# A batched expert MLP on one Trainium2 core: x by one transfer of 32 KB rows, prepared by quarter of its columns and token parity

## The chip, the cores and the metric

The kernel runs on one core of one Trainium2 chip. The metric is the device time of one execution in microseconds (us), the median of several executions. TensorE (PE) multiplies, ScalarE (ACT) and VectorE (DVE) copy, cast and apply relu, GpSimd (POOL) and SyncE (SP) issue the transfers here.

## The reference

```python
# n_experts 8, capacity 256, hidden 512, expert_hidden 2048; all float32
def reference(x, w1, w2):            # x [8,256,512], w1 [8,512,2048], w2 [8,2048,512]
    h = np.matmul(x, w1)
    h = np.maximum(h, 0)
    return np.matmul(h, w2).astype(np.float32)
```

The weights are 67.1 MB of float32, x and the output 4.19 MB each. The kernel multiplies in bfloat16.

## The kernel before

Each expert has two weight matrices of 4.19 MB. GpSimd loads each by one transfer (the last w2 by two, of 9 and 7 of its 16 rows per partition), and the transfer casts float32 to bfloat16: one row of 32 KB of float32 for each of 128 partitions. There are two buffers for w1 (`w1_sb`) and two for w2 (`w2_sb`), one for even and one for odd experts.

The experts go in pairs. For a pair TensorE does layer 1 of the even expert, layer 1 of the odd one, then layer 2 of the even and of the odd one. Layer 1 of an expert is 128 matmuls into `ph` (L272); ACT and DVE take turns to apply relu into `ht` (L219, L221). Layer 2 is 32 matmuls into `po` (L292), which ACT and DVE copy to `o_sb` (L228).

The order of transfers is GpSimd's program. First come the third single expert of x (expert 3, L142), x of experts 4 to 7 with a cast (`x_c`, L143), w1 of experts 0 and 1, w2 of experts 0 and 1. Then, for each later pair, it waits until layer 1 of an expert is through (`s_first`, L161) and reloads that w1 buffer, and until layer 2 of an expert is copied out (`s_act`, L164) and reloads that w2 buffer. So w1 of expert 2 is issued when layer 1 of expert 0 has ended, and all that GpSimd issues stands in one queue in this order. At the end GpSimd writes the output of experts 0 to 3 (L167), and SyncE that of 4 to 6 and of 7 (L126, L128). SyncE also tells TensorE when weights are there (`t_w`, L106 to L124): for the first layers it waits until x of that expert is prepared (`s_xe`) and until w1 has landed.

x must have its hidden dimension on the partitions. This is done before the first layer, in four rounds. In a round DVE (b=0) and ACT (b=1) each cast 128 tokens' worth of rows, 1024 elements in each partition, into `x_b` (`cast`, L178); TensorE transposes 16 blocks of 128x128 into `pt` (L256); DVE and ACT each copy 1024 elements in each partition from `pt` into `xe` (L194, L198). A round's transposes wait for both casts, a copy for its eight transposes, and the next cast of an engine stands behind its copy. One round prepares two experts, so the first layer of expert 0 needs the first round alone; but TensorE's program has the four rounds ahead of all layers.

x comes by four transfers: expert 0 (512 KB, SyncE), experts 1 and 2 (1 MB, SyncE), expert 3 (512 KB, GpSimd), all float32 in `x_f`, and experts 4 to 7 (2 MB of float32, landing as bfloat16 in `x_c`, GpSimd). In each partition the rows of a transfer are 4, 8, 4 and 16 KB of float32. The copies to `xe` write runs of contiguous elements for experts 0 and 3 (L194), every second element for 1 and 2, every fourth for 4 to 7 (L198).

Of the kernel before, what the change touches and what calls it, by code (L numbers as in the profile page):

```python
# [9 lines left out]
def kernel(  # L10
# [7 lines left out]
    nc = tc.nc  # L18
    P = 128
    bf = mybir.dt.bfloat16  # L20
    f32 = mybir.dt.float32
    relu = mybir.ActivationFunctionType.Relu

    E, C, H = x.shape
    F = w1.shape[2]
    MT = C // P
    KT1 = H // P
# [3 lines left out]
    G = E // 2  # L31
# [6 lines left out]

    J = G * MT
    x_r = x.rearrange("e (p m) k -> p e m k", m=MT)
    x_pair = x[1:3].rearrange("e c k -> (e c) k").rearrange("(p s m) k -> p s m k", p=P, m=MT)
    x_rows = x[G:].rearrange("e c k -> (e c) k").rearrange("(p j) k -> p j k", p=P)


    x_f = nc.alloc_sbuf_tensor("x_f", [P, G, MT, H], f32)
    x_c = nc.alloc_sbuf_tensor("x_c", [P, J, H], bf)
    x_b = nc.alloc_sbuf_tensor("x_b", [P, 2, KT1 * MT, P], bf)
    xe = nc.alloc_sbuf_tensor("xe", [P, E * KT1 * C], bf)  # L50
    w1_sb = nc.alloc_sbuf_tensor("w1_sb", [P, 2 * KT1 * F + KT2], bf)
# [9 lines left out]
    pt = [nc.alloc_psum_tensor(f"pt_tr{b}", [P, KT1 * MT, P], bf) for b in range(2)]  # L61

    sem = nc.alloc_semaphore
    s_x = [sem(f"s_x{i}") for i in range(3)]
    s_xc = sem("s_xc")
    s_out = [sem(f"s_out{i}") for i in range(3)]
    s_w1 = [sem(f"s_w1_{e}") for e in range(E)]
    s_w2 = [sem(f"s_w2_{e}") for e in range(E)]
# [10 lines left out]
    t_xb = sem("t_xb")  # L79
    s_xe = [sem(f"s_xe{b}") for b in range(2)]  # L80
# [4 lines left out]
    sp, pool, act, dve, pe = nc.sync, nc.gpsimd, nc.scalar, nc.vector, nc.tensor  # L85
# [3 lines left out]

    def load_x(eng, e, n, src, i):
        ins = eng.dma_start(x_f[:, e:e + n], src).then_inc(s_x[i], 16)
        return ins.ins.name

    tc.no_tile_sem_insts.add(load_x(sp, 0, 1, x_r[:, :1], 0))
    tc.no_tile_sem_insts.add(load_x(sp, 1, 2, x_pair, 1))
    tc.close()
    tc.compile()  # L99

    def copied(eng, n):
        eng.wait_ge(s_act, n)
        eng.wait_ge(s_dve, n)


    for e in range(0, E, 2):  # L106
        for b in range(2):

            if e < G:
                sp.wait_ge(s_xe[b], e // 2 + 1)  # L110
                if e + b == 1:
                    sp.wait_ge(s_xe[0], 2)
            elif e + b == G:
                for s in s_xe:
                    sp.wait_ge(s, G)
            sp.wait_ge(s_w1[e + b], 16).then_inc(t_w, 1)
        for b in range(2):
            if b:
                copied(sp, e + 1)
            if e + b < E - 1:  # L120
                sp.wait_ge(s_w2[e + b], 16).then_inc(t_w, 2)
            else:
                sp.wait_ge(s_w2[e + b], 16).then_inc(t_w, 1)
                sp.wait_ge(s_w2b, 16).then_inc(t_w, 1)  # L124
# [6 lines left out]
    def load_w1(e):  # L131
        pool.dma_start(w1_k[:, e % 2 * KT1:(e % 2 + 1) * KT1], w1_r[e]).then_inc(s_w1[e], 16)  # L132

    def load_w2(e):
# [3 lines left out]
        else:  # L138
            pool.dma_start(w2_k[:, k:k + CUT], w2_r[e, :, :CUT]).then_inc(s_w2[e], 16)  # L139
            pool.dma_start(w2_k[:, k + CUT:k + KT2], w2_r[e, :, CUT:]).then_inc(s_w2b, 16)  # L140

    load_x(pool, G - 1, 1, x_r[:, G - 1:G], 2)  # L142
    pool.dma_start(x_c[:], x_rows).then_inc(s_xc, 16)  # L143
    load_w1(0)
    load_w1(1)
    pool.memset(identity[:], 0.0).then_inc(s_id, 1)
# [23 lines left out]

    def cast(eng, r, b):

        a = 2 * r + b
        src = x_f[:, a] if a < G else x_c[:, MT * (a - G):MT * (a - G + 1)]
        copy = act.copy if eng is act else dve.tensor_copy
        copy(  # L178
            x_b[:, b].rearrange("p (t m) q -> p t m q", m=MT),
            src.rearrange("p m (q t) -> p t m q", t=KT1),  # L180
        ).then_inc(t_xb, 1)

    def take_x(eng, b):
        copy = act.copy if eng is act else dve.tensor_copy
        for r in range(G):
            if r < G // 2:
                eng.wait_ge(s_x[(2 * r + b + 1) // 2], 16)
            elif r == G // 2:
                eng.wait_ge(s_xc, 16)
            cast(eng, r, b)  # L190
            eng.wait_ge(s_tr, 2 * r + b + 1)
            a, n = 2 * r + b, KT1 * C
            if a in (0, G - 1):
                copy(xe[:, a * n:(a + 1) * n], pt[b][:].rearrange("p j q -> p (j q)")).then_inc(s_xe[b], 1)  # L194
            else:
                e0, l = (1, 2) if a < G else (G, G)
                xl = xe[:, e0 * n:(e0 + l) * n].rearrange("p (l j q f) -> p l j q f", l=l, j=KT1 * MT, f=l)
                copy(  # L198
                    xl[:, :, :, :, a - e0].rearrange("p l j q -> p j l q"),
                    pt[b][:].rearrange("p j (l q) -> p j l q", l=l),  # L200
                ).then_inc(s_xe[b], 1)

# [25 lines left out]

    act.sem_inc(t_ha, 1)
    take_x(act, 1)
    layers(act, 1, s_ha, s_oa, t_ha, s_act)

    dve.sem_inc(t_hb, 1)
    take_x(dve, 0)
    layers(dve, 0, s_hb, s_ob, t_hb, s_dve)

# [13 lines left out]
    with pe.Fori(0, G) as _r:  # L252
        take(t_xb, 2)
        for b in range(2):
            for j in range(KT1 * MT):
                ins = pe.transpose(pt[b][:, j], x_b[:, b, j], identity[:])  # L256
            ins.then_inc(s_tr, 1)

    with pe.Fori(0, G) as g:
        with pe.Fori(0, 2) as b:  # L260
            xs = ahead(xe, False, g * (4 * KT1 * C) + b * (2 * KT1 * C), [kt * C for kt in range(KT1)], C)
            take(t_w)
            with pe.Fori(0, NQ) as q:
                for i in range(FB):
# [6 lines left out]
                    for kt in range(KT1):  # L271
                        ins = pe.matmul(  # L272
                            ph[i // 2][:, i % 2, :],
                            ws[i % 2 * KT1 + kt],
                            xs[kt],
                            start=(kt == 0),
                            stop=(kt == KT1 - 1),
                        )
                    if i % 2:
                        ins.then_inc((s_hb, s_ha)[i // 2], 1)  # L280
        with pe.Fori(0, 2) as b:
            for kt in range(KT2):
# [8 lines left out]
                for m in range(MT):  # L291
                    ins = pe.matmul(  # L292
                        po[:, m],
                        hs[(kt - k0) * MT + m],
                        ws[kt - k0],
                        start=(kt == 0),
                        stop=(kt == KT2 - 1),
                    )
# [35 lines left out]
```

## Time and profile before

| | |
|---|---|
| time of three executions | 179.56, 179.69, 179.77 us; median 179.69 |
| span of the profiled execution | 178.3 us, so 1.4 us of the median lie outside it |
| mean granted TensorE clock | 0.966 of full speed |
| PE, ACT, DVE busy | 73%, 21%, 21% of the span |
| read from and written to HBM | 71.30 MB, 4.19 MB: 423 GB/s over the span |

The profile is of one execution; its own time is its span. Busy time is per engine. A share of DMA is the mean over 16 DMA engines. A transfer that casts is counted by the bytes that it writes, half of those that it reads, so 217 GB/s of a casting transfer are 433 GB/s of float32. Durations of DMA_DIRECT2D are those of issuing; the time "to landing" runs from the issue to the arrival of the last byte.

### The profile page before, as it was taken

Reading aid. Unit: us, or ns where it says so; the run is one execution under the profiler, and the core shown is the slowest. Engines: PE = TensorE matmul, PEld = TensorE weight load, DVE = VectorE, ACT = ScalarE, POOL = GpSimd, SP = SyncE. Lnnn points to the kernel's source line nnn. Section 1 sums busy time; section 2 is a strip of 40 time slices with the busy share of each in tenths; the row PEclk is TensorE's granted clock in tenths of the full one; section 3 lists DMA queues with packets and bytes.
Section 4 is the critical chain, followed back from the end, with each engine's and each line's share of the span. In section 5 each row is a group of like instructions: output and inputs, shape, how many; then the busy total and the mean of one; then the engine's idle time right before and its main releaser. Section 6 shows DMA issues by size and latency. Waiting matters only on the chain. (4 is left out here: it accounts for less than half of the span.)

```text
span 178.3 us, 2360 instructions
## 1 busy us (share of the span) xinstructions
PE 130.5 (73%) x832; PEld 88.8 (50%) x832; DVE 37.6 (21%) x48; ACT 37.9 (21%) x49; POOL 12.3 (7%) x26
## 2 busy tenths in 40 slices
PE   0034479899939296888769695979496698999880
PEld 0033378785414195873224485954142587964330
DVE  0134654331010133330100231320101113410110
ACT  2455554232010122130100132220101022220110
POOL 3600000101010101000000101010101200000000
PEclk9999999999999999999969999999999569999997
DMA  5999999999999998998998998999999999999998
GB/s 232 327 217 224 235 198 213 235 202 210 235 213 198 235 221 191 235 224 191 232 228 191 228 232 191 224 232 202 213 235 202 210 235 213 198 218 208 270 421 353
DMA packets 4096, 40.90 MB, mean 229 GB/s; under 512 B 384, under 2 KB 384, under 8 KB 1792
## 3 DMA queue, kind: packets, MB, share of 16 engines
q0 software_dynamic: 3264, 37.23, 95.1%
q1 hardware_dynamic: 832, 3.67, 5.1%
HBM read 71.30 MB, written 4.19 MB: 423 GB/s over the span
## 5 line engine op out<-in xcount | busy, mean ns | idle before, releaser
L272 PE MATMUL pt_h<-xe,w_sb 128*128 x512 | 65.1, 283 | 13.0 <-PEq L88 13.0
L272 PEld LDWEIGHTS pt_h<-xe,w_sb 128*128 x512 | 57.4, 147 | 21.3 <-issue 19.5
L292 PE MATMUL pt_o<-w_sb,ht_sb 128*128 x256 | 58.2, 387 | 11.9 <-PEq L88 11.8
L292 PEld LDWEIGHTS pt_o<-w_sb,ht_sb 128*128 x256 | 24.9, 99 | 44.2 <-issue 16.9
L221 DVE TENSOR_SCALAR ht_sb<-pt_h 128x512 bf16<-128x512 f32 x32 | 22.2, 692 | 52.0 <-PE pt_h L272 52.0
L219 ACT ACTIVATE ht_sb<-pt_h 128x512 bf16<-128x512 f32 x32 | 19.2, 600 | 57.0 <-PE pt_h L272 57.0
L256 PE MATMUL pt_tr<-identity,x_b 128*128 128x128 bf16 x64 | 7.5, 309 | 17.8 <-PEq L88 17.8
L228 DVE COPY out_sb<-pt_o 128x512 f32 x8 | 5.5, 691 | 67.2 <-PE pt_o L292 67.2
L228 ACT COPY out_sb<-pt_o 128x512 f32 x8 | 4.7, 585 | 65.4 <-PE pt_o L292 65.4
L256 PEld LDWEIGHTS pt_tr<-identity,x_b 128*128 128x128 bf16 x64 | 6.5, 143 | 18.5 <-issue 18.5
L132 POOL DMA_DIRECT2D w_sb<-in_w_dram x8 | 4.9, 612 | 70.1 <-ACTq L223 70.1
L198 DVE COPY xe<-pt_tr 128x1024 bf16<-128x1024 bf16 x3 | 6.3, 2091 | 8.1 <-PE pt_tr L256 8.1
L198 ACT COPY xe<-pt_tr 128x1024 bf16<-128x1024 bf16 x3 | 6.3, 2085 | 6.1 <-PE pt_tr L256 6.1
L137 POOL DMA_DIRECT2D w_sb<-in_w_dram x7 | 3.7, 534 | 44.5 <-ACT out_sb L228 44.4
L178 ACT CAST x_b<-x_f 128x1024 bf16<-128x1024 f32 x2 | 4.0, 1984 | 3.0 <-DMA x_f<-in_x_dram 3.0
L178 DVE CAST x_b<-x_f 128x1024 bf16<-128x1024 f32 x2 | 2.1, 1064 | 4.1 <-DMA x_f<-in_x_dram 4.1
L178 ACT COPY x_b<-x_c 128x1024 bf16<-128x1024 bf16 x2 | 2.2, 1117 | 0.0
L178 ACT ACT_TABLE_LOAD x1 | 1.3, 1283 | 2.5 <-PEq L99 2.5
L194 DVE COPY xe<-pt_tr 128x1024 bf16<-128x1024 bf16 x1 | 0.7, 691 | 4.7 <-PE pt_tr L256 4.7
L194 ACT COPY xe<-pt_tr 128x1024 bf16<-128x1024 bf16 x1 | 1.0, 1012 | 2.0 <-PE pt_tr L256 2.0
L178 DVE COPY x_b<-x_c 128x1024 bf16<-128x1024 bf16 x2 | 1.4, 692 | 0.0
L139 POOL DMA_DIRECT2D w_sb<-in_w_dram x1 | 0.5, 528 | 9.2 <-ACT out_sb L228 9.2
(10 smaller groups left out, 3.4 us busy)
## 6 DMA issues: line engine op xcount, KB each, us to landing
w_sb<-in_w_dram POOLq DMA_DIRECT2D x15, 2048.0 KB, 29.9
out_dram<-out_sb POOLq DMA_DIRECT2D x1, 2048.0 KB, 35.9
out_dram<-out_sb SPq DMA_DIRECT2D x1, 1536.0 KB, 8.6
w_sb<-in_w_dram POOLq DMA_DIRECT2D x1, 1152.0 KB, 26.4
x_f<-in_x_dram SPq DMA_DIRECT2D x1, 1024.0 KB, 5.5
x_c<-in_x_dram POOLq DMA_DIRECT2D x1, 1024.0 KB, 9.3
w_sb<-in_w_dram POOLq DMA_DIRECT2D x1, 896.0 KB, 30.4
x_f<-in_x_dram SPq DMA_DIRECT2D x1, 512.0 KB, 3.3
```

The costliest lines, as they stand in the source:

```text
L132: pool.dma_start(w1_k[:, e % 2 * KT1:(e % 2 + 1) * KT1], w1_r[e]).then_inc(s_w1[e], 16)
L137: pool.dma_start(w2_k[:, k:k + KT2], w2_r[e]).then_inc(s_w2[e], 16)
L139: pool.dma_start(w2_k[:, k:k + CUT], w2_r[e, :, :CUT]).then_inc(s_w2[e], 16)
L178: copy(x_b[:, b].rearrange("p (t m) q -> p t m q", m=MT), src.rearrange("p m (q t) -> p t m q", t=KT1),).then_inc(t_xb, 1)
L194: copy(xe[:, a * n:(a + 1) * n], pt[b][:].rearrange("p j q -> p (j q)")).then_inc(s_xe[b], 1)
L198: copy(xl[:, :, :, :, a - e0].rearrange("p l j q -> p j l q"), pt[b][:].rearrange("p j (l q) -> p j l q", l=l),).then_inc(s_xe[b], 1)
L219: act.activation(dst, ph[half][:], relu).then_inc(t_h, 1)
L221: dve.tensor_relu(dst, ph[half][:]).then_inc(t_h, 1)
L228: copy(outs[b], po[:, half]).then_inc(s_copied, 1)
L256: ins = pe.transpose(pt[b][:, j], x_b[:, b, j], identity[:])
L272: ins = pe.matmul(ph[i // 2][:, i % 2, :], ws[i % 2 * KT1 + kt], xs[kt], start=(kt == 0), stop=(kt == KT1 - 1),)
L292: ins = pe.matmul(po[:, m], hs[(kt - k0) * MT + m], ws[kt - k0], start=(kt == 0), stop=(kt == KT2 - 1),)
```

## The change

All of x comes by one SyncE transfer of 128 rows of 32 KB, as float32, into `x_f`. Partition p holds 16 consecutive tokens of expert p // 16. GpSimd issues no x any more, so w1 of expert 0 is its first transfer. Round r now takes the columns of x with remainder r by 4, of all experts; DVE takes even and ACT odd tokens. All casts read float32. The copies read `pt` with a step of 128 elements in runs of 8, and write contiguous runs of 128 elements. Every round writes a part of every expert, so SyncE waits for all four rounds of both engines before it lets the first layer of expert 0 begin.

```diff
-    J = G * MT
-    x_r = x.rearrange("e (p m) k -> p e m k", m=MT)
-    x_pair = x[1:3].rearrange("e c k -> (e c) k").rearrange("(p s m) k -> p s m k", p=P, m=MT)
-    x_rows = x[G:].rearrange("e c k -> (e c) k").rearrange("(p j) k -> p j k", p=P)
+    J = E * MT
+    x_rows = x.rearrange("e c k -> (e c) k").rearrange("(p j) k -> p j k", p=P)
-    x_f = nc.alloc_sbuf_tensor("x_f", [P, G, MT, H], f32)
-    x_c = nc.alloc_sbuf_tensor("x_c", [P, J, H], bf)
+    x_f = nc.alloc_sbuf_tensor("x_f", [P, J, H], f32)
...
-    tc.no_tile_sem_insts.add(load_x(sp, 0, 1, x_r[:, :1], 0))
-    tc.no_tile_sem_insts.add(load_x(sp, 1, 2, x_pair, 1))
+    tc.no_tile_sem_insts.add(sp.dma_start(x_f[:], x_rows).then_inc(s_x, 16).ins.name)
...
-            if e < G:
-                sp.wait_ge(s_xe[b], e // 2 + 1)
-                if e + b == 1:
-                    sp.wait_ge(s_xe[0], 2)
-            elif e + b == G:
+            if e + b == 0:
                 for s in s_xe:
                     sp.wait_ge(s, G)
...
-    load_x(pool, G - 1, 1, x_r[:, G - 1:G], 2)
-    pool.dma_start(x_c[:], x_rows).then_inc(s_xc, 16)
     load_w1(0)
...
+    x_by = x_f[:].rearrange("p (f m) (q t) -> p t m f q", m=MT, t=KT1)
+    xe_by = xe[:].rearrange("p (l t m q f) -> p t m l q f", l=E, t=KT1, m=MT, f=E)
+
     def cast(eng, r, b):
-
-        a = 2 * r + b
-        src = x_f[:, a] if a < G else x_c[:, MT * (a - G):MT * (a - G + 1)]
         copy = act.copy if eng is act else dve.tensor_copy
-        copy(
-            x_b[:, b].rearrange("p (t m) q -> p t m q", m=MT),
-            src.rearrange("p m (q t) -> p t m q", t=KT1),
-        ).then_inc(t_xb, 1)
+        copy(x_b[:, b], x_by[:, r, b]).then_inc(t_xb, 1)
...
         for r in range(G):
-            if r < G // 2:
-                eng.wait_ge(s_x[(2 * r + b + 1) // 2], 16)
-            elif r == G // 2:
-                eng.wait_ge(s_xc, 16)
+            if r == 0:
+                eng.wait_ge(s_x, 16)
             cast(eng, r, b)
             eng.wait_ge(s_tr, 2 * r + b + 1)
-            a, n = 2 * r + b, KT1 * C
-            if a in (0, G - 1):
-                copy(xe[:, a * n:(a + 1) * n], pt[b][:].rearrange("p j q -> p (j q)")).then_inc(s_xe[b], 1)
-            else:
...
+            copy(xe_by[:, r, b], pt[b][:].rearrange("p f (l q) -> p l q f", l=E)).then_inc(s_xe[b], 1)
```

## Rows read from the trace of the kernel before

**Rows 1.** The page: DMA share in 40 slices of the span, and HBM traffic.
```profile
DMA  5999999999999998998998998999999999999998
HBM read 71.30 MB, written 4.19 MB: 423 GB/s over the span
```
**Rows 2.** DMA issues, KB each, us to landing; min/median/max of L137.
```profile
x_c<-in_x_dram POOLq DMA_DIRECT2D x1, 1024.0 KB, 9.3
...
w_sb<-in_w_dram POOLq DMA_DIRECT2D x1, 2048.0 KB, 18.5
...
w_sb<-in_w_dram POOLq DMA_DIRECT2D x1, 2048.0 KB, 27.5
...
w_sb<-in_w_dram POOLq DMA_DIRECT2D x1, 2048.0 KB, 30.6
...
DMA to landing us min/median/max: 28.9/30.6/44.5
...
out_dram<-out_sb SPq DMA_DIRECT2D x1, 512.0 KB, 4.3
```
**Rows 3.** Timeline of the issues: start us, us, engine line.
```profile
0.74 0.86 SPq L93 DMA_DIRECT2D x_f<-in_x_dram  x2
2.92 0.67 POOL L93 DMA_DIRECT2D x_f<-in_x_dram  x1 [2.48 <-POOLq L99]
3.59 0.55 POOL L143 DMA_DIRECT2D x_c<-in_x_dram  x1
4.11 1.71 POOL L132 DMA_DIRECT2D w_sb<-in_w_dram  x2
6.68 1.09 POOL L137 DMA_DIRECT2D w_sb<-in_w_dram  x2
...
33.88 0.53 POOL L132 DMA_DIRECT2D w_sb<-in_w_dram  x1 [26.11 <-ACTq L223]
...
127.57 0.53 POOL L137 DMA_DIRECT2D w_sb<-in_w_dram  x1 [8.43 <-ACT out_sb L228]
...
168.43 0.40 SPq L126 DMA_DIRECT2D out_dram<-out_sb  x1
...
173.91 0.35 SPq L128 DMA_DIRECT2D out_dram<-out_sb  x1
```
**Rows 4.** Timeline of layers on PE: expert 0, 1 and 2, then 6 and 7.
```profile
25.09 2.39 PE L272 MATMUL pt_h<-xe,w_sb 128*128 x16
27.70 5.83 PE L272 MATMUL pt_h<-xe,w_sb 128*128 x48 [0.21 <-PEq L88]
...
51.86 7.07 PE L292 MATMUL pt_o<-w_sb,ht_sb 128*128 x32 [2.69 <-PEq L88]
...
62.16 7.77 PE L272 MATMUL pt_h<-xe,w_sb 128*128 x64 [3.23 <-PEq L88]
...
139.60 10.26 PE L272 MATMUL pt_h<-xe,w_sb 128*128 x64 [3.18 <-PEq L88]
...
150.47 7.77 PE L272 MATMUL pt_h<-xe,w_sb 128*128 x64 [0.62 <-PEq L88]
...
158.34 7.07 PE L292 MATMUL pt_o<-w_sb,ht_sb 128*128 x32
...
166.19 7.07 PE L292 MATMUL pt_o<-w_sb,ht_sb 128*128 x32 [0.79 <-PEq L88]
```
**Rows 5.** Stretches: us, busy us (count) of five engines, PEclk, DMA share, GB/s.
```profile
0.00:1.75 1.75, 0.00 (x0) 0.00 (x0) 0.00 (x0) 0.00 (x0) 0.20 (x4) 1.00 0.00 0
1.75:2.75 1.00, 0.00 (x0) 0.00 (x0) 0.00 (x0) 0.29 (x1) 0.00 (x0) 1.00 0.77 287
4.50:6.00 1.50, 0.00 (x0) 0.00 (x0) 0.66 (x1) 0.00 (x0) 1.50 (x3) 1.00 0.92 377
139.50:149.90 10.40, 10.26 (x64) 8.47 (x64) 2.77 (x4) 1.80 (x4) 0.00 (x0) 0.71 0.98 208
177.00:178.30 1.30, 0.00 (x0) 0.00 (x0) 0.00 (x0) 0.00 (x0) 0.00 (x0) 0.50 0.45 183
```
**Rows 6.** ACT and PE in the first rounds, timeline: start us, us.
```profile
6.71 1.98 ACT L178 CAST x_b<-x_f 128x1024 bf16<-128x1024 f32 x1 [2.96 <-DMA x_f<-in_x_dram]
8.83 1.86 PE L256 MATMUL pt_tr<-identity,x_b 128*128 128x128 bf16 x16 [8.83 <-PEq L88]
10.73 1.30 ACT L198 COPY xe<-pt_tr 128x1024 bf16<-128x1024 bf16 x1 [2.04 <-PE pt_tr L256]
11.90 1.98 ACT L178 CAST x_b<-x_f 128x1024 bf16<-128x1024 f32 x1
...
25.34 2.52 ACT L198 COPY xe<-pt_tr 128x1024 bf16<-128x1024 bf16 x1 [2.05 <-PE pt_tr L256]
```
**Rows 7.** Groups by line and shape: casts and copies of x, mean ns of one.
```profile
L178 ACT CAST x_b<-x_f 128x1024 bf16<-128x1024 f32 x2 | 4.0, 1984 | 3.0 <-DMA x_f<-in_x_dram 3.0
L178 DVE CAST x_b<-x_f 128x1024 bf16<-128x1024 f32 x2 | 2.1, 1064 | 4.1 <-DMA x_f<-in_x_dram 4.1
L178 ACT COPY x_b<-x_c 128x1024 bf16<-128x1024 bf16 x2 | 2.2, 1117 | 0.0
L194 ACT COPY xe<-pt_tr 128x1024 bf16<-128x1024 bf16 x1 | 1.0, 1012 | 2.0 <-PE pt_tr L256 2.0
```
**Rows 8.** DMA queues in 3.6:5.7: packets, MB, share of 16 engines (q1 SyncE's).
```profile
q1 hardware_dynamic: 106, 0.86, 99.7%
```
**Rows 9.** DMA queues in 169.45:171.95 (q0 is GpSimd's).
```profile
q0 software_dynamic: 257, 1.05, 102.2%
```

More of the change, by code (lines that the diff above doesn't have):

```diff
@@ L63 @@
     sem = nc.alloc_semaphore
-    s_x = [sem(f"s_x{i}") for i in range(3)]
-    s_xc = sem("s_xc")
+    s_x = sem("s_x")
     s_out = [sem(f"s_out{i}") for i in range(3)]
@@ L88, in take @@
         pe.wait_ge(s, n).then_inc(s, -n)
-    def load_x(eng, e, n, src, i):
-        ins = eng.dma_start(x_f[:, e:e + n], src).then_inc(s_x[i], 16)
-        return ins.ins.name
-    tc.no_tile_sem_insts.add(load_x(sp, 0, 1, x_r[:, :1], 0))
-    tc.no_tile_sem_insts.add(load_x(sp, 1, 2, x_pair, 1))
+    tc.no_tile_sem_insts.add(sp.dma_start(x_f[:], x_rows).then_inc(s_x, 16).ins.name)
     tc.close()
@@ L185, in take_x @@
         for r in range(G):
-            if r < G // 2:
-                eng.wait_ge(s_x[(2 * r + b + 1) // 2], 16)
-            elif r == G // 2:
-                eng.wait_ge(s_xc, 16)
+            if r == 0:
+                eng.wait_ge(s_x, 16)
             cast(eng, r, b)
             eng.wait_ge(s_tr, 2 * r + b + 1)
-            a, n = 2 * r + b, KT1 * C
-            if a in (0, G - 1):
-                copy(xe[:, a * n:(a + 1) * n], pt[b][:].rearrange("p j q -> p (j q)")).then_inc(s_xe[b], 1)
-            else:
[L196 to L201, printed above, removed]
+            copy(xe_by[:, r, b], pt[b][:].rearrange("p f (l q) -> p l q f", l=E)).then_inc(s_xe[b], 1)
     def layers(eng, half, s_h, s_o, t_h, s_copied):
```

## The prediction

> **What bounds the kernel now.** I read the page's slices first. From the second slice on the DMA engines are busy nine tenths or more of every slice, while the two directions of HBM traffic sum to 423 GB/s [rows 1]. The reader is to see that no compute engine fills the span, and that the transfers do. Next come the landings. The first w1 is issued at 4.11 and lands 18.5 later, at 22.6; w2 of expert 1 is the second issue of its line, at 6.68 + 0.55 = 7.2, and lands 44.5 later, at 51.7 [rows 2, 3]. Between them lie three weight transfers in 29.1 us, so one takes 9.7. x before it ended at 3.59 + 9.3 = 12.9, which is 9.7 ahead of 22.6: the transfers run nose to tail.
>
> Then I asked what ties the end to that queue, by the timeline. w2 of expert 6 lands at 127.57 + 30.6 = 158.17, and its layer 2 starts at 158.34. Layer 2 of expert 7 follows at 166.19 and ends at 173.26; the last output is issued at 173.91 and needs 4.3 [rows 2 to 4]. So the end is the landing of that w2 and some 20 us that the change doesn't touch. TensorE is only just in time there: layer 1 of expert 7 ends at 150.47 + 7.77 = 158.24, 0.1 ahead of the start of layer 2 [rows 4].
>
> So x matters in two ways: how long its 4.19 MB hold the DMA engines ahead of the weights, and whether its preparation becomes so late that a weight buffer is freed after the queue has run dry.
>
> **The change part by part.** *Bytes.* x is read as float32 before and after, 4.19 MB, as much as a weight transfer; at the pace above that is 9.7 us. Before, it took from 1.75, where the DMA engines begin [rows 5], to 12.9: 11.15, or 1.45 more. Of these, two things stay. The engines start one after the other (share 0.77 in the first microsecond, 0.23 lost). And landing comes after the last byte: of the last 1.3 us of the span the engines are busy 0.45, so they stop on average at 177.6, while the landing is at 173.91 + 4.3 = 178.2, a lag of 0.6 [rows 2, 3, 5]. That leaves at most 1.45 - 0.23 - 0.6 = 0.6 to gain. The least is the hole where SyncE's part hands over to GpSimd's: a share of 0.92 over 1.5 us, 0.12 [rows 5]. In between lies the price of short rows: the output's 4 KB rows move 1.05 MB in 2.5 us, 420 GB/s [rows 9], against 4.19 MB in 9.7 us, 432, for the weights' 32 KB rows, 3% more; on 9.7 us that is 0.27, a bound since some rows of x are longer. I take 0.12 + 0.27 = 0.4, with 0.1 and 0.6 as ends.
>
> *Issues.* SyncE issues one transfer in place of two, at 0.74 as now. GpSimd drops two issues of 0.67 and 0.55 [rows 3], so w1 comes into its queue 1.2 earlier. I cost this at nothing: x still occupies the engines then. If that cover were gone, 1.2 would be the gain.
>
> *x as a whole.* Preparation can't begin before all of x is there. I let x run alone, to 12.9 - 0.4 = 12.5, because of two stretches. From 3.6 to 5.7 only SyncE's queue moves, with GpSimd's first x issued at 2.92; from 169.45 to 171.95 only GpSimd's queue moves, with a SyncE transfer issued at 168.43 [rows 3, 8, 9]. Who comes second waits.
>
> *Casts.* All eight read float32 with a step of four elements. On ACT that took 1984 ns against 1117 from bfloat16, on DVE 1064 [rows 7]; ACT sets the round.
>
> *Copies.* Writes become contiguous, reads have a step of 128. No row shows such a read. The contiguous copy took 1.01 on ACT, the one with every fourth element written 2.52 [rows 6, 7]. The nearest row is ACT's cast, which reads single elements 16 bytes apart and takes 1.98; I take 2.0, with 1.0 and 2.5 as ends. The Trainium skill (SBUF — State Buffer, the section on the DMA port swizzle, Door 1) says that PSUM has lines of 8 bytes, half of SBUF's, and that patterns which are not contiguous cost there; by it every element read is a line of its own, and 2.0 rather than 1.0 is what the sum would use. No row yet bears on its PSUM half.
>
> *A round.* From ACT's first cast to its second, 6.71 to 11.90, are 5.19, with a copy of 1.30 in it [rows 6]; the rest is 3.89. Four rounds of 3.89 + 2.0 are 23.6, so preparation ends at 12.5 + 23.6 = 36.1. From a landed w1 to the first matmul pass 0.8 (33.88 + 27.5 = 61.4, then 62.16 [rows 2 to 4]): layer 1 of expert 0 begins at 36.9, not at 25.09.
>
> *The reissue.* Behind SyncE's new wait stand all of TensorE's layers, behind these GpSimd's next w1. It came 33.88 - 25.09 = 8.8 after the first matmul; a layer 1 in a stretch with a granted clock of 0.71 took 10.26 against 7.77 [rows 3 to 5], so 11.3 is the other end. The first sixteen matmuls took 2.39, where a quarter of 7.77 is 1.94, so some of that already happens there; with copies standing between the last transposes and the matmuls I take 10.0. The reissue falls at 46.9, ends 41.5 and 50.5.
>
> *Its deadline.* w2 of expert 1 would land at 51.7 - 0.4 = 51.3, its engines stop 0.6 earlier, at 50.7. From issue to first byte are 1.0 for SyncE's first transfer (0.74 to 1.75), at most 2.8 for GpSimd's (2.92 to past 5.7); I take 2.0, so the issue is due at 48.7. There are 1.8 to spare, and the lateness costs nothing while w2 of expert 1 covers it. From then on the deadlines recede: layers of 7.8 and 7.1 with gaps under 0.8 come faster than transfers of 9.7, so TensorE makes up its 11.8 within the next two pairs, well ahead of the tail.
>
> **Sum.** The queue ends 0.4 earlier and nothing else lies on its path. The span of the profiled execution becomes 177.9; the 1.4 outside make it 179.3, which is also the median less 0.4.
>
> **Rivals.** *The queues share.* The Trainium skill (DMA: Bandwidth & Descriptors, Issuing engines are not separate DMA queues) says that transfers of different issuers interleave on the same engines. The two stretches above speak against it [rows 8, 9]. As a mechanism: by 5.8 each engine has moved three of its eight rows of x (1.21 each, an eighth of 9.7); the other five alternate with four rows of w1 and end at 5.8 + 9 x 1.21 = 16.7, landing 0.6 later at 17.3. The reissue moves to 51.7, its bytes to 53.7, and 3.0 of idle DMA make 179.3 + 3.0 = 182.3. Faster copies (1.0) with the short layer would still save it, at 46.5. Chance 0.15.
>
> *The copy out of PSUM is slower still.* This one mechanism makes the change slower: from a copy of 2.46 on (12.5 + 4 x 6.35 + 0.8 + 10.0 = 48.7) the reissue misses its deadline and the DMA engines stand idle around 50. At all the dear ends it comes at 50.5, its bytes at 53.3, 2.6 late: 181.9. For it speaks that single elements are dear in every row; against it, that the dear copies wrote with steps and these don't. Chance 0.12.
>
> *Nothing is gained.* A 32 KB row as float32 fills SBUF with twice the bytes of a cast one, and may move no faster than x did; or TensorE's 0.1 of reserve at 158.24 goes, if a stretch of lower clock falls otherwise. Then 179.7. For it: the gain is read out of small holes. Chance 0.15.
>
> **How the numbers follow.** The forecast has 0.58, with a range of its own of 179.1 to 179.6. A measurement of this kernel tells 0.2%, 0.36 us, from no change. The forecast's gain passes that in about seven of ten cases: 0.41 faster, 0.17 same; the third rival gives 0.14 same, 0.01 slower; the two gaps, 0.27, give 0.05 same, 0.01 faster, 0.21 slower. Sums: 0.42, 0.36, 0.22. The range runs from 179.0 (a gain of 0.6 and the spread of 0.1 of the runs) to 181.9, the dear end of the second rival, and leaves out the worse half of the sharing.
>
> **What would show it.** Right: DMA share of nine tenths through 40 to 60 us; x landing near 12.5, 11.8 after its issue; w1 landing near 22.2; ACT's copies near 2.0; layer 1 of expert 0 from 36.9; layer 2 of expert 6 near 157.9. Wrong: x landing past 16, an ACT copy over 2.4, or a hole in the DMA share about 50 with every later landing late by its length.

## The result and the profile after

The kernel after takes 181.82 us (four runs, 181.44 to 182.09), the kernel before in the same comparison 179.62: a ratio of 1.0122, 95% interval 1.011 to 1.0134. It is slower by 2.2, where 0.4 faster (179.3) was forecast. That 181.82 still lies under the dear end of the forecast's range, 181.9, is luck: that end was priced from dear copies out of PSUM, and these turned out cheap. The span of the profiled execution is 180.7, 2.4 above the one before.

The page of the kernel after, its DMA share in 40 slices and its HBM traffic, against [rows 1]:
```profile
DMA  6999999999899999999999999999999999999996
HBM read 71.30 MB, written 4.19 MB: 418 GB/s over the span
```
The same bytes move, and the slices show nothing of the loss: the one eight covers 45.2 to 49.7 us, before the place that counts, and the kernel before has five eights. The place shows in the timeline of the kernel after (start us, us, engine), against [rows 3, 4, 6]:
```profile
0.74 0.38 SPq L88 DMA_DIRECT2D x_f<-in_x_dram  x1
2.43 1.21 POOL L119 DMA_DIRECT2D w_sb<-in_w_dram  x2 [1.98 <-POOLq L90]
...
18.97 2.00 ACT L163 CAST x_b<-x_f 128x1024 bf16<-128x1024 f32 x1 [15.71 <-DMA x_f<-in_x_dram]
...
23.93 1.99 ACT L163 CAST x_b<-x_f 128x1024 bf16<-128x1024 f32 x1
...
37.85 1.01 ACT L172 COPY xe<-pt_tr 128x1024 bf16<-128x1024 bf16 x1 [2.05 <-PE pt_tr L227]
39.69 9.47 PE L243 MATMUL pt_h<-xe,w_sb 128*128 x64 [1.88 <-PEq L84]
...
49.51 0.53 POOL L119 DMA_DIRECT2D w_sb<-in_w_dram  x1 [43.92 <-ACTq L194]
...
128.96 0.53 POOL L124 DMA_DIRECT2D w_sb<-in_w_dram  x1 [8.46 <-ACT out_sb L199]
...
159.73 7.07 PE L263 MATMUL pt_o<-w_sb,ht_sb 128*128 x32 [1.39 <-PEq L84]
...
175.30 0.34 SPq L115 DMA_DIRECT2D out_dram<-out_sb  x1
```
ACT waits for x until 18.97. Four rounds follow, the first of 4.96 (18.97 to 23.93), and layer 1 of expert 0 begins at 39.69, where before it began at 25.09 [rows 4]. (The row has all of its matmuls: layer 1 of an expert is 64, not 128 as said above.) The next w1 is issued at 49.51, not at 33.88 [rows 3]. The issues of the kernel after, KB each and us to landing, in this order x, w1 of expert 0, w1 of expert 2, w2 of expert 6 and the last output, against [rows 2]:
```profile
x_f<-in_x_dram SPq DMA_DIRECT2D x1, 4096.0 KB, 18.2
...
w_sb<-in_w_dram POOLq DMA_DIRECT2D x1, 2048.0 KB, 20.1
...
w_sb<-in_w_dram POOLq DMA_DIRECT2D x1, 2048.0 KB, 13.1
...
w_sb<-in_w_dram POOLq DMA_DIRECT2D x1, 2048.0 KB, 30.6
...
out_dram<-out_sb SPq DMA_DIRECT2D x1, 512.0 KB, 5.4
```
x lands at 0.74 + 18.2 = 18.9, and w1 of expert 2 at 49.51 + 13.1 = 62.6, where before it was 33.88 + 27.5 = 61.4: 1.2 late. w2 of expert 6 lands at 128.96 + 30.6 = 159.56, 1.4 late. The last output is issued 1.4 late and takes 5.4 in place of 4.3; so 1.4 of the loss come with the weights, and 1.1 at the very end.

Who used the DMA engines while x was on its way shows in the queues of the kernel after from 7 to 17 us (q0 GpSimd's, q1 SyncE's: packets, MB, share of 16 engines), where before only one queue moved at a time in the stretches that the prediction read [rows 8, 9]:
```profile
q0 software_dynamic: 65, 1.06, 49.8%
q1 hardware_dynamic: 64, 2.10, 49.0%
```
65 packets against 64: each engine takes a row of w1 and a row of x in turn, half of the time each. The 64 rows of x are four of the eight that each engine has; the first four went alone. The turns show in short windows, 15.7 to 16.3, 16.3 to 18.1 and 18.1 to 18.7:
```profile
q1 hardware_dynamic: 16, 0.52, 204.3%
...
q0 software_dynamic: 16, 0.26, 68.1%
...
q0 software_dynamic: 16, 0.26, 204.3%
q1 hardware_dynamic: 16, 0.00, 3.7%
```
Sixteen last rows of x, one per engine, begin by 16.3 and take 1.2. Then come sixteen rows of w1, and only behind these sixteen packets of a few bytes, with which the transfer of x reports that it is complete. So the report had to wait for a turn too: the last row of x was through by 17.5, and ACT learnt of it at 18.97.

DMA share from 49 to 57 us, in 40 slices of 0.2, of the kernel after:
```profile
DMA  0009990000999059400399783399737399737399
```
A packet of 1.2 us is counted where it starts, so a queue that runs without gaps shows groups of nines 1.2 apart. The first group is the last rows of w2 of expert 1. The second, from 51.0, is already the reissued w1: eleven engines begin it by 51.6, and five more between 51.8 and 52.4.

### The profile page after: what moved, and what is told of

Read it like the earlier page. It is cut to its first block, busy times and chain, and to the rows that moved or that the text cites. A ratio compares the mean times of both kernels' runs of the same rounds, so it can differ in the third digit from the quotient of the medians.

```text
span 180.7 us, 2356 instructions
## 1 busy us (share of the span) xinstructions
PE 127.1 (70%) x832; PEld 87.9 (49%) x832; DVE 36.6 (20%) x48; ACT 36.8 (20%) x49; POOL 10.6 (6%) x24
## 5 line engine op out<-in xcount | busy, mean ns | idle before, releaser
L243 PE MATMUL pt_h<-xe,w_sb 128*128 x512 | 63.7, 280 | 9.5 <-PEq L84 9.5
L243 PEld LDWEIGHTS pt_h<-xe,w_sb 128*128 x512 | 56.8, 146 | 16.9 <-issue 15.7
L263 PE MATMUL pt_o<-w_sb,ht_sb 128*128 x256 | 56.5, 379 | 7.7 <-PEq L84 7.7
L163 ACT CAST x_b<-x_f 128x1024 bf16<-128x1024 f32 x4 | 8.0, 1991 | 15.7 <-DMA x_f<-in_x_dram 15.7
L163 DVE CAST x_b<-x_f 128x1024 bf16<-128x1024 f32 x4 | 4.3, 1064 | 19.0 <-DMA x_f<-in_x_dram 19.0
L172 DVE COPY xe<-pt_tr 128x1024 bf16<-128x1024 bf16 x4 | 4.9, 1225 | 10.3 <-PE pt_tr L227 10.3
L172 ACT COPY xe<-pt_tr 128x1024 bf16<-128x1024 bf16 x4 | 4.0, 1012 | 8.2 <-PE pt_tr L227 8.2
L152 POOL DMA_DIRECT2D out_dram<-out_sb x1 | 0.8, 763 | 0.0
## 6 DMA issues: line engine op xcount, KB each, us to landing
x_f<-in_x_dram SPq DMA_DIRECT2D x1, 4096.0 KB, 18.2
```

Of the source, the lines that this page charges most:

```text
L152: pool.dma_start(out_r[:, :G], o_sb[:, :G]).then_inc(s_out[0], 16)
L163: copy(x_b[:, b], x_by[:, r, b]).then_inc(t_xb, 1)
L172: copy(xe_by[:, r, b], pt[b][:].rearrange("p f (l q) -> p l q f", l=E)).then_inc(s_xe[b], 1)
L243: ins = pe.matmul(ph[i // 2][:, i % 2, :], ws[i % 2 * KT1 + kt], xs[kt], start=(kt == 0), stop=(kt == KT1 - 1),)
L263: ins = pe.matmul(po[:, m], hs[(kt - k0) * MT + m], ws[kt - k0], start=(kt == 0), stop=(kt == KT2 - 1),)
```

## The experiments

**Half of x on GpSimd.** Each half is 16 KB of a row of x; GpSimd's goes ahead of the weights. The preparation by quarters stays.
```diff
-    tc.no_tile_sem_insts.add(sp.dma_start(x_f[:], x_rows).then_inc(s_x, 16).ins.name)
+    tc.no_tile_sem_insts.add(sp.dma_start(x_f[:, :J // 2], x_rows[:, :J // 2]).then_inc(s_x[0], 16).ins.name)
...
+    pool.dma_start(x_f[:, J // 2:], x_rows[:, J // 2:]).then_inc(s_x[1], 16)
     load_w1(0)
...
-                eng.wait_ge(s_x, 16)
+                for s in s_x:
+                    eng.wait_ge(s, 16)
```


> The kernel after, but only the first half of each 32 KB row of x goes by SyncE; GpSimd brings the second half ahead of the first w1. The preparation by quarters stays. Theory (rows of x and of w1 took turns, x came too late, the weight queue ran dry): x lands at about 13, preparation takes 20.7 from there as in the profile after, layer 1 of expert 0 begins at 33.7, the next w1 is issued at about 43.5 and no hole appears: 179.4 to 179.8, two under the kernel after. Rival (the loss lies in the new preparation, in filling SBUF with float32 or at the end): 181 or more.

Measured: ratio to the kernel before 0.9998 (0.9989 to 1.0007), median 179.50. GpSimd's half was issued at 2.44 and landed 10.6 later, at 13.0; layer 1 of expert 0 began at 35.07, the next w1 was issued at 45.11 and landed 16.3 later, at 61.4, as before. The new preparation, all casts from float32 and a first layer 10 later than before cost nothing; what costs is x beside the weights. DMA share from 49 to 57 of this kernel:
```profile
DMA  0009990009990003993003993000993000993000
```
The groups of nines go through 51 without a break.

**w1 of expert 0 in short rows.** The kernel after, with x untouched:
```diff
-    load_w1(0)
+    for k in range(KT1):
+        pool.dma_start(w1_k[:, k:k + 1], w1_r[0, :, k:k + 1]).then_inc(s_w1[0], 16)
...
-            sp.wait_ge(s_w1[e + b], 16).then_inc(t_w, 1)
+            sp.wait_ge(s_w1[e + b], 16 if e + b else 16 * KT1).then_inc(t_w, 1)
```


> The kernel after, with w1 of expert 0 alone brought by four transfers with rows of 8 KB in place of one with rows of 32 KB. Theory (each DMA engine takes one row of SyncE's queue and one of GpSimd's in turn, however long): the four rows of x left at 6.8 wait 0.31 each and not 1.21, x lands at about 13, no hole at 50, 179.4 to 179.8. Rival (the queues share by bytes or by time): x lands near 19 as in the kernel after, 181.8.

Measured: ratio 1.0004 (0.9995 to 1.0013), median 179.66. Its x, and its queues from 8 to 12.5:
```profile
x_f<-in_x_dram SPq DMA_DIRECT2D x1, 4096.0 KB, 13.8
```
```profile
q1 hardware_dynamic: 47, 1.54, 80.0%
q0 software_dynamic: 48, 0.20, 21.5%
```
One row for one row again, and now x has 80% of the time, as 32 KB has beside 8 KB. x landed at 0.74 + 13.8 = 14.5, later than the 13 expected, and the next w1 was issued at 45.07. The same bytes on the same queues, with four transfers in place of one, take the whole loss away.

**x in short rows.** The other way round:
```diff
-    tc.no_tile_sem_insts.add(sp.dma_start(x_f[:], x_rows).then_inc(s_x, 16).ins.name)
+    for j in range(0, J, 4):
+        tc.no_tile_sem_insts.add(sp.dma_start(x_f[:, j:j + 4], x_rows[:, j:j + 4]).then_inc(s_x, 16).ins.name)
...
-                eng.wait_ge(s_x, 16)
+                eng.wait_ge(s_x, 64)
```


> The kernel after, with x brought by four SyncE transfers whose rows are 8 KB. Theory (one row from each queue in turn): half of x is there when w1 begins at 6.8; the other 16 rows of each engine wait 1.21 each and move in 0.31, so x lands near 31; layer 1 of expert 0 begins at 52, the next w1 is issued near 62 and the engines are idle for some 13: about 193 to 195. Rival (sharing by bytes or time): x lands near 19, 181.8.

Measured: ratio 1.0837 (1.0818 to 1.0857), median 194.59, inside the expectation. The queues from 9 to 30:
```profile
q0 software_dynamic: 240, 3.67, 81.8%
q1 hardware_dynamic: 240, 1.79, 21.1%
```
240 against 240: equal numbers of rows, and x gets a fifth of the time. The first cast waited until 32.37, the next w1 was issued at 63.65. Sharing by bytes or by time is ruled out by the two runs together.

**The kernel before, held.** x and its preparation as before; SyncE holds the first layer until a later weight has landed (w2 of expert 0; in the next run w1 of expert 1):
```diff
                 sp.wait_ge(s_xe[b], e // 2 + 1)
+                if e + b == 0:
+                    sp.wait_ge(s_w2[0], 16)
```


> The kernel before, but SyncE holds the first layer of expert 0 until w2 of expert 0 has landed, at 41.9; x and its preparation are untouched. Theory (a late reissue of w1 costs the time that the DMA engines stand idle): first matmul at 42.7, reissue at 52.2, bytes at 54.2 against engines that run dry at 50.7: 3.5 lost, 183 to 184. Rival (TensorE makes the delay up, the loss lies in x's transfer or preparation): 179.6 to 180.0.

Measured: ratio 1.0263 (1.0248 to 1.0279), median 184.36, 0.4 above the expectation. The first matmul came at 42.74 as expected, the next w1 was issued at 53.15 and not at 52.2, and it landed 12.6 later, at 65.7, 4.4 late. Its DMA share from 49 to 57 shows the hole bare:
```profile
DMA  0079930000000000000000000009990000079793
```

> The kernel before, but SyncE holds the first layer of expert 0 until w1 of expert 1 has landed, at 32.3. Theory (lateness is free until the weight queue runs dry): first matmul at 33, next w1 issued near 43, before the deadline of 48.7, so 179.5 to 179.7. Rival (each microsecond of lateness of the first layer costs): with some 8 late, 181 or more.

Measured: ratio 1.0000 (0.9991 to 1.0009), median 179.64. The first layer began at 33.09 and the next w1 was issued at 43.12; 8 us of lateness were free.

**Held to the reissue of the kernel after.** w2 of expert 0 in two transfers, the first layer held for the first of them:
```diff
+        if e == 0:
+            pool.dma_start(w2_k[:, :11], w2_r[0, :, :11]).then_inc(s_hold, 16)
+            pool.dma_start(w2_k[:, 11:KT2], w2_r[0, :, 11:]).then_inc(s_w2[0], 16)
...
+                if e + b == 0:
+                    sp.wait_ge(s_hold, 16)
```


> The kernel before, with w2 of expert 0 brought by two transfers (11 and 5 of its 16 rows) and the first layer of expert 0 held until the first of them has landed, near 38.9. That puts the next w1 where the kernel after has it, near 49.6, with the old transfers and preparation of x. Theory (the whole loss hangs on this late issue, the part that appears only at the end too): 181.4 to 182.1. Rival (only the 1.25 by which that w1 landed late hangs on it, the other 1.1 comes from x's transfer or preparation): 180.5 to 181.0.

> The kernel after once more, on the same chip as the held kernel, for its profile. Every theory expects 181.4 to 182.1 and w1 of expert 2 to land near 62.6; if the last output again takes 5.4 rather than 4.3 from its issue, the tail belongs to this kernel and not to one execution.

Measured: the held kernel 181.15 (ratio 1.0073, 1.0048 to 1.0099; its runs lie between 179.85 and 181.89), between the two expectations; the kernel after again 182.20 (1.0135, 1.0113 to 1.0156). In the profiled executions the held kernel issued the next w1 at 50.17 and had a span of 180.6, the kernel after at 50.25 and 180.9. At equal reissue the spans agree within 0.3, with the last output taking 4.5 and 4.8 from its issue. But the profiled execution of the held kernel is the slowest of its six (181.89), so this agreement is of one execution each. The medians leave room for up to some 1 us that only the kernel after has; its x came at 0.74 + 19.5 = 20.2 in this execution and at 18.9 in the other, so its reissue may lie later on average. That wasn't separated further.

**Short rows at the restart.** The held kernel that took 184.36, with w1 of expert 2 in four transfers:
```diff
     def load_w1(e):
+        if e == 2:
+            for k in range(KT1):
+                pool.dma_start(w1_k[:, k:k + 1], w1_r[e, :, k:k + 1]).then_inc(s_w1[e], 16)
+            return
...
-            sp.wait_ge(s_w1[e + b], 16).then_inc(t_w, 1)
+            sp.wait_ge(s_w1[e + b], 16 * KT1 if e + b == 2 else 16).then_inc(t_w, 1)
```


> The kernel before held until w2 of expert 0 has landed, as in the run that took 184.36, but w1 of expert 2 is issued as four transfers with rows of 8 KB. Theory (besides the idle time, the first long row on each restarted engine takes up to 2.5 in place of 1.23): 0.4 to 0.8 less than there, 183.5 to 184.0. Rival (only the idle time counts): 184.3 to 184.5.

Measured: ratio 1.0221 (1.0191 to 1.0251), median 183.17, more than expected. But its first layer took 9.03 against 10.06 in the other, and the reissue came at 52.08 and not 53.15, which alone is 1.1 of the 1.2. From the reissue to the landing of the following w1, of expert 3, it took 60.35 + 13.9 - 52.08 = 22.2 against 61.41 + 14.3 - 53.15 = 22.6. So short rows at the restart may be worth 0.4; one execution of each doesn't prove it.

**Short first rows of x.** The kernel with half of x on GpSimd, and SyncE's half cut in two (the edit is shown against the kernel after):
```diff
-    tc.no_tile_sem_insts.add(sp.dma_start(x_f[:], x_rows).then_inc(s_x, 16).ins.name)
+    for i, (j, n) in enumerate(((0, 2), (2, 6))):
+        tc.no_tile_sem_insts.add(sp.dma_start(x_f[:, j:j + n], x_rows[:, j:j + n]).then_inc(s_x[i], 16).ins.name)
...
+    pool.dma_start(x_f[:, J // 2:], x_rows[:, J // 2:]).then_inc(s_x[2], 16)
     load_w1(0)
```


> The kernel with the second half of x on GpSimd, and SyncE's half in two transfers: first 4 KB, then 12 KB of each row of x. Theory (the forecast 0.4 was lost because the first 32 KB row on each engine took 1.9 on average against 1.23 later; short first rows don't pay that): w1 of expert 0 lands 0.3 earlier than the 22.6 of the kernel before, 179.2 to 179.3. Rival (the start costs the same whatever the rows): 179.5 to 179.6.

Measured: ratio 1.0003 (0.9994 to 1.0013), median 179.69. w1 of expert 0 landed at 3.59 + 18.9 = 22.5, not 0.3 earlier. The theory of the first rows falls; no version tried is faster than the kernel before.

## Why the prediction was wrong

The step that failed is *x as a whole*: "I let x run alone". x landed at 18.9 and not at 12.5, and so the reissue came at 49.51, past its deadline of 48.7; with x at 13.0 and at 14.5 it came at 45.1, and nothing was lost. The two stretches [rows 8, 9] showed that a second queue begins late, and I read from that that it waits until the first is through. The row that tells the two apart stood right behind: from 172 to 174 us of the kernel before, when SyncE's output had begun, both queues move.
```profile
q1 hardware_dynamic: 145, 0.59, 72.0%
q0 software_dynamic: 76, 0.25, 30.3%
```
GpSimd's transfer runs out in this stretch, so the counts aren't equal. And at the start SyncE's x was nearly through when GpSimd's first row came, so nothing could be seen of what follows. In the kernel after w1 was issued at 2.43 and moved nothing until 7.2, then took every second turn. The Trainium skill (DMA: Bandwidth & Descriptors, Issuing engines are not separate DMA queues), as the first rival cites it, was right that the queues interleave; the trace agrees, 65 packets against 64.

Point by point:

- *Bytes.* This step failed too, though it isn't what made the kernel slower. The gain of 0.4 isn't there: w1 of expert 0 landed at 2.43 + 20.1 = 22.5, against 22.6. The 0.12 of a hand-over was a misreading. A packet is counted where it starts, so the share of 0.92 from 4.5 to 6 [rows 5] follows one of 1.09, and the two make 3.29 in 3.25 us, without a hole. The first line is this stretch of the kernel before, the second has the first rows of x in the kernel after, 1.7 to 2.5 us:
```profile
2.75:4.50 1.75, 0.00 (x0) 0.00 (x0) 0.41 (x1) 0.99 (x1) 1.58 (x3) 1.00 1.09 445
...
q1 hardware_dynamic: 16, 0.52, 231.3%
```
  The sixteen first rows of 32 KB took 1.85 each (2.313 x 0.8), where later ones take 1.23: 0.6 lost on each engine, more than the longer rows were to bring. Cutting the first rows short gained no time either. Why the start costs the same in both is open.
- *Copies.* Mis-sized: 2.0 taken on ACT, 1.01 measured. The groups by line of the kernel after (mean ns of one), against [rows 7]:
```profile
L163 ACT CAST x_b<-x_f 128x1024 bf16<-128x1024 f32 x4 | 8.0, 1991 | 15.7 <-DMA x_f<-in_x_dram 15.7
L172 DVE COPY xe<-pt_tr 128x1024 bf16<-128x1024 bf16 x4 | 4.9, 1225 | 10.3 <-PE pt_tr L227 10.3
L172 ACT COPY xe<-pt_tr 128x1024 bf16<-128x1024 bf16 x4 | 4.0, 1012 | 8.2 <-PE pt_tr L227 8.2
```
  On ACT a step of 128 elements out of PSUM costs what a contiguous read does, 1012 [rows 7]. On DVE it took 1225 against 691 for its contiguous copy before, but ACT sets the round. The Trainium skill (SBUF — State Buffer, Door 1: The DMA port swizzle), by which the lines of PSUM were to speak for 2.0, says of matmuls that such patterns slow them; ACT's copy doesn't follow it, and the measurement decides. The second rival, a dearer copy, is out.
- *A round, the hand-over and the reissue* held: 3.89 + 1.01 is 4.90 against 4.96, the first matmul follows the last copy by 0.8, and the reissue the first matmul by 9.8, where 10.0 was taken. The 10.0 is luck in part. It was taken between 8.8 and an end read from a granted clock of 0.71 [rows 5]; here the layer took 9.5 with the granted clock at 1.00, so something else made it long:
```profile
39.69:49.20 9.51, 9.46 (x64) 8.01 (x64) 2.77 (x4) 1.80 (x4) 0.00 (x0) 1.00 1.03 221
```
- *Its deadline* held. A w1 issued into a dry queue lands 12.4 to 13.1 later, so to land at 61.4, as before, it must be issued by 48.8 (61.4 - 12.6); the prediction had 48.7. The runs, with the reissue in the profiled execution:

| kernel | reissue of w1, us | ratio to before |
|---|---|---|
| before | 33.88 | 1 |
| held to w1 of expert 1 | 43.12 | 1.0000 |
| half of x on GpSimd, short first rows | 45.05 | 1.0003 |
| w1 in short rows | 45.07 | 1.0004 |
| half of x on GpSimd | 45.11 | 0.9998 |
| after | 49.51 | 1.0122 |
| held to a part of w2 | 50.17 | 1.0073 |
| after, again | 50.25 | 1.0135 |
| held, w1 of expert 2 in short rows | 52.08 | 1.0221 |
| held to w2 of expert 0 | 53.15 | 1.0263 |
| x in short rows | 63.65 | 1.0837 |

  Up to 45.1 lateness is free; at 63.65, 14.9 past the deadline, 15.0 are lost (0.0837 x 179.56).
- *The first rival, the queues share,* is what happened, with its own sizes off in both directions. Its rows of x end at 16.7 and did end by 17.5, but it left out that the report of completion waits for a turn as well, so x landed at 18.9 and not at 17.3. The copy was too dear, by 4.0 over four rounds. 3.0 of hole were priced, 1.2 came with the first landing.

The loss at the restart is not idle time alone. Each transfer ends with sixteen packets of a few bytes, as many as there are engines. Those of w2 of expert 1 and the first rows of the next w1 stand together in the queue of the kernel before from 50.5 to 51.4, and of the kernel after from 50.5 to 51.6 and from 51.6 to 52.4:
```profile
q0 software_dynamic: 32, 0.26, 138.7%
...
q0 software_dynamic: 27, 0.18, 120.6%
...
q0 software_dynamic: 5, 0.08, 62.6%
```
Before, the sixteen rows take 1.23 each (1.387 x 0.9, less the small packets). After, eleven begin by 51.6 and five later, and they take 1.8 on average (1.206 x 1.1 + 0.626 x 0.8). By the starts of all packets in the trace an engine is idle for 0.4 on average. So the slow first rows, 0.6, cost more than the hole itself.

The unequal restart stays to the end. Completions (the packets under 512 B) of w2 of expert 6, in the kernel before from 157.2 to 157.9, in the kernel after from 158.2 to 158.8 and from 158.8 to 159.3:
```profile
DMA packets 32, 0.15 MB, mean 211 GB/s; under 512 B 16, under 2 KB 16, under 8 KB 16
...
DMA packets 22, 0.10 MB, mean 169 GB/s; under 512 B 11, under 2 KB 11, under 8 KB 11
DMA packets 19, 0.13 MB, mean 258 GB/s; under 512 B 5, under 2 KB 5, under 8 KB 5
```
By their times, they spread over 0.6 us in every weight transfer of the kernel before; in the kernel after over 0.5 up to the restart and over 1.0 from there to the last half of the last w2. Those of w2 of expert 6 are 1.1 late on average, and its landing, for which TensorE waits, 1.4.

At the end more is added. Windows of the kernel after (us, busy us of the engines, clock, DMA share, GB/s), against 177.0 to 178.3 before [rows 5]:
```profile
177.00:179.40 2.40, 0.00 (x0) 0.00 (x0) 0.00 (x0) 0.00 (x0) 0.00 (x0) 0.50 0.87 355
179.40:180.70 1.30, 0.00 (x0) 0.00 (x0) 0.00 (x0) 0.00 (x0) 0.00 (x0) 0.50 0.10 41
```
By these shares the engines stop on average at 177.0 + 2.09 + 0.13 = 179.2, 1.6 later than before (177.6), while the last byte comes 2.5 later (180.7 against 178.2): three of the sixteen completions of the last output come after 180.0. So 0.5 on average is added behind the 1.1 of the restart. It lies in rows of the last half of the last w2, here of the kernel after from 166 to 168 us and of the kernel before from 164 to 166:
```profile
q0 software_dynamic: 44, 0.32, 114.2%
...
q0 software_dynamic: 58, 0.42, 106.8%
```
These rows take 0.83 and 0.59 each. Summed over the transfer, they take 0.9 and 0.4 per engine more than at the 0.55 that undisturbed ones need. In the other traces it is 0.0 to 0.4 where the queue stayed full and 0.4 to 0.6 where it ran dry, one execution of each; its cause is open.

## What to carry to other kernels

In these kernels SyncE's and GpSimd's transfers took turns row by row, so a transfer's share was set by its row length against the other's: give the urgent one long rows and what runs beside it short ones, or put the urgent one ahead in the same queue. A later start of the compute engines was free here as long as the weight queue held work (reissues up to 45.1); write down when a buffer must be freed for the queue not to run dry, and check a change against that time. A stretch in which one queue alone moves says nothing of who goes first once the other has begun; look for a stretch in which both have work.

## What the runs showed of the hardware that was not expected

Turns go by packet: 65 to 64, 48 to 47 and 240 to 240 for rows (w1 to x) of 32 to 32, 8 to 32 and 32 to 8 KB. The few bytes that report a transfer complete wait for a turn as well: 1.2 us behind a 32 KB row of w1. The first 32 KB rows on idle engines took 1.85 at the start of the kernel after and 1.8 at 51 us, against 1.23 in a running queue. And GpSimd's first w1, issued at 2.43, moved nothing until 7.2, so a transfer that stands first in its queue can still leave its neighbour 4.8 us alone.
